# Four small constants' loads moved in SP's order, and a head selector made on ScalarE, in an RWKV-7 layer

## The chip, the core and the metric

The kernel runs on one core of a Trainium2 chip (trn2). The metric is device time in microseconds for one execution, lower is better. Engines are named as in the profile: PE is TensorE, ACT ScalarE, DVE VectorE, POOL GpSimd, and SP the sync engine, whose queue issues nearly all of this kernel's DMAs.

## The reference, cut to what matters

One decoder layer over 2048 tokens of width 1024, in float32: RWKV-7 time mixing with 12 heads of 64, beside a 4-head cross-attention into 256 memory tokens, then a squared-ReLU MLP of width 4096.

```python
h = rms_norm(x, norm_mix_g)
proj = h @ rw_in                                   # (2048, 2816)
slab = token_shift(proj[..., :2560], rw_mu)        # z + (z_prev - z) * mu
r, k, v, wd, ad, gd = split(slab)
...                                                # decay, a, g by small loras; kk normalised per head
y = delta_rule_scan(r, decay, k, v, -kk, kk * a)   # 2048 steps, 12 heads
mix = (group_norm(y) + bonus) * g
mem_out = memory_cross_attention(q_mem, k_mem, v_mem, ...)
x = x + concat([mix, mem_out]) @ w_out
x = x + square(relu(rms_norm(x, norm_ffn_g) @ w_ff1)) @ w_ff2
```

## The kernel before

Tokens come in four groups of 512 and in 16 pairs of chunks of 64. `project(g)` (L633) brings a group's x in four tiles of 128 rows, normalises them (`rows_norm`, L148: a square with its sum on ACT, L151; a reciprocal root on POOL, L86; a scaling on DVE, L153), transposes them on PE (L161) and splits them into a high and a low part, `xh` on ACT (L92) and `xl` on DVE (L93). It then multiplies with the 22 blocks of 128 columns of `rw_in`: 24 matmuls of 128 x 512 for a block (L102, three for each of eight slices of the inner width). For the first group, the weights of a block come as four loads `ws` (L604), are scaled by the gain `gmc` and split into `w` (ACT L95, DVE L96), and are stored for the later groups as `w_d` (L609). The buffers of `w` hold two blocks, so the split of block b waits for the matmuls of block b - 2.

A finished block `pz` leaves PSUM in `shift_store` (L666): ACT scales it by `omc` = 1 - mu (L674), DVE adds the shifted part with `muc` = mu (L675) and keeps the last column (L680), and the result `sl` is stored as `rk_d` (L682). The pool `psx` that holds `pz` has three banks, and the transposes of the memory tokens (`memory_setup`, L710: tiles `mt`, transposed as `pt`, split as `mh` and `ml`) take banks of the same pool in between. After five blocks stand the projections of the memory tokens to keys and values, `pk` (L628), with weights `wo` scaled by `gm`.

The constants: `gmc`, `gm` and `gfc` (L170) are gains of 1024 values, loaded as 128 partitions of 8 single values; `muc` (L575) is 2560 values as 128 partitions of 20, and `omc` is made of it on DVE (L577). `gm` is first needed by the memory weights, `gfc` by the MLP's rows (L849). The head selector `sel2` (12 heads by 768 columns, in three parts at partitions 96, 64 and 0) is written in `scan_setup` on POOL: a memset of one and two selections for each part (L231 to L235). The identity `ident` is made on POOL too. `sel2` is first read by a matmul at L356, in the first pair's preparation.

The order on each engine is set by a scheduler that runs over the whole program: it takes what is ready on its own estimate of times, lowest rank (`tc.cur_priority`) first, so one moved rank can change the order of much that follows. The DMAs that SP issues use eight completion semaphores in turn: in the program, a DMA's issue also waits until the one eight places ahead of it has landed.

Of the kernel before, what the change touches and what calls it, by code (L numbers as in the profile page):

```python
# [13 lines left out]
ALU = mybir.AluOpType  # L14
# [11 lines left out]
MW = 768  # L26
NB = MW // P
NH = 12
HD = 64
# [31 lines left out]
def hybrid_layer(  # L61
# [6 lines left out]
    nc = tc.nc  # L68
# [7 lines left out]
    ident = cst.tile([P, P], F32, name="ident")  # L76
# [91 lines left out]
    def gain_col(pool, src, name):  # L168
        t = pool.tile([P, KB], F32, name=name)
        nc.sync.dma_start(t, src.rearrange("(k p) -> p k", p=P))  # L170
        return t
# [17 lines left out]
    def col(src, name):  # L189
        t = cb.tile([P, NB], F32, name=name)  # L190
        nc.sync.dma_start(t, src.rearrange("(b p) -> p b", p=P))
        return t
# [3 lines left out]
    heads = lambda a: a.rearrange("p (h d) -> p h d", d=HD)  # L196
# [4 lines left out]
    def scan_setup():  # L201
        K["kkc"] = col(rw_k_k[0], "kkc")
        kac = col(rw_k_a[0], "kac")
        K["lbc"] = col(rw_lnx_b[0], "lbc")
        K["ka2"] = ka2 = cb.tile([P, NB], F32, name="ka2")
        nc.vector.tensor_scalar_mul(ka2, kac, 0.5)
        K["ka1"] = ka1 = cb.tile([P, NB], F32, name="ka1")
        nc.vector.tensor_scalar(ka1, kac, -0.5, 1.0, ALU.mult, ALU.add)
        K["lgr"] = lgr = cb.tile([P, MW], F32, name="lgr")
        nc.sync.dma_start(lgr, rw_lnx_g.to_broadcast([P, MW]))  # L210

        K["lora"], K["lob"] = [], []
        for which, (w2, w0) in enumerate(((rw_w2, rw_w0), (rw_a2, rw_a0))):
            src = pr.tile([P, MW], F32, tag="kk", name="lsrc")
            for o in range(2):
                nc.sync.dma_start(src[o * HD : (o + 1) * HD], w2[0])
            wt = cb.tile([P, MW], F32R, name=f"lora{which}")
            lo = pr.tile([P, MW], F32R, tag="EM", name="llo")
            nc.scalar.copy(wt[:HD], src[:HD])
            nc.scalar.copy(lo[HD:], src[HD:])  # L220
            nc.vector.tensor_tensor(wt[HD:], src[HD:], lo[HD:].bitcast(F32), op=ALU.subtract)
            K["lora"].append(wt)
            b0 = col(w0[0], f"lob{which}")
            nc.vector.tensor_scalar_mul(b0, b0, 0.5)
            K["lob"].append(b0)

        K["sel2"] = sel2 = cb.tile([96 + NH, MW], BF16, name="sel2")
        nc.gpsimd.memset(sel2, 0.0)
        for o in PARTS:
            so = sel2[o : o + NH]  # L230
            nc.gpsimd.memset(so, 1.0)  # L231
            nc.gpsimd.affine_select(so, so, pattern=[[1, MW]], compare_op=ALU.is_ge,
                                    fill=0.0, base=0, channel_multiplier=-HD)
            nc.gpsimd.affine_select(so, so, pattern=[[-1, MW]], compare_op=ALU.is_ge,
                                    fill=0.0, base=HD - 1, channel_multiplier=HD)  # L235
        K["rn3"] = rn3 = cb.tile([96 + NH, P], BF16, name="rn3")
        nc.gpsimd.memset(rn3, 0.0)
        K["g2s"] = g2s = cb.tile([P, MW], F32, name="g2s")
        nc.sync.dma_start(g2s, rw_g2[0])
        K["rkm"] = rkm = cb.tile([P, NB, 2], F32, name="rkm")  # L240
        nc.vector.memset(rkm, 0.0)
        rk_src = rw_r_k[0].rearrange("(b two) d -> two d b", two=2)
        nc.sync.dma_start(rkm[:HD, :, 0], rk_src[0])
        nc.sync.dma_start(rkm[HD:, :, 1], rk_src[1])

        K["sel1"] = sel1 = cb.tile([P, NB * NH], F32, name="sel1")
        nc.vector.memset(sel1, 0.0)
        nc.vector.memset(sel1[:HD, 0 : 14 * NB - 13 : 14], 1.0)
        nc.vector.memset(sel1[HD:, 1 : 14 * NB - 12 : 14], 1.0)

        K["msk"] = msk = cb.tile([P, P], F32, name="msk")
        nc.gpsimd.memset(msk, 1.0)
        nc.gpsimd.affine_select(msk[:HD, :C], msk[:HD, :C], pattern=[[1, C]], compare_op=ALU.is_ge,
                                fill=0.0, base=-1, channel_multiplier=-1)
        nc.gpsimd.affine_select(msk[:HD, C:], msk[:HD, C:], pattern=[[1, C]], compare_op=ALU.is_ge,
                                fill=0.0, base=0, channel_multiplier=-1)
        nc.sync.dma_start(msk[HD:], msk[:HD])
        K["rst"] = rst = cb.tile([P, 2 * P], F32, name="rst")
        nc.vector.memset(rst, 1.0)
        nc.vector.memset(rst.rearrange("p (a c) -> p a c", c=C)[:, :, 0], 0.0)  # L260

        zrow = K["zrow"] = dram.tile([2, 512], F32, name="zrow")
        ztmp = pr.tile([1, 512], F32, tag="zt", name="ztmp")
        for par in range(2):
            nc.vector.memset(ztmp, 0.0)
            nc.vector.memset(ztmp[:, par : 512 : 34], 1.0)
            nc.sync.dma_start(zrow[par : par + 1], ztmp)
        K["E"] = cb.tile([P, NB, 2, C + 1], F32, name="E")

        K["Z"] = [cb.tile([P, NB, 2 * C], F32, name=f"Z{i}") for i in range(3)]  # L270
        K["te2"] = [cb.tile([P, NB, 32], F32, name=f"te2{i}") for i in range(2)]
        nc.vector.memset(K["E"][:, :, :, 0], 1.0)
        for t in K["Z"] + K["te2"]:
            nc.gpsimd.memset(t, 0.0)
        S = st.tile([P, NB, HD], F32, tag="S", name="S")
        nc.vector.memset(S, 0.0)
        return S
# [291 lines left out]
    wp = astk.enter_context(tc.tile_pool(name="a_w", bufs=WBUF))  # L569
    ep = astk.enter_context(tc.tile_pool(name="a_e", bufs=2))  # L570
    gmc = gain_col(xp, g_mix[0], "gmc")
    gm = gain_col(xp, g_mem, "gm")
    gfc = gain_col(xp, g_ffn[0], "gfc")
    muc = xp.tile([P, 20], F32, name="muc")
    nc.sync.dma_start(muc, rw_mu[0].rearrange("(b p) -> p b", p=P))  # L575
    omc = xp.tile([P, 20], F32, name="omc")
    nc.vector.tensor_scalar(omc, muc, -1.0, 1.0, ALU.mult, ALU.add)  # L577
    last = [xp.tile([P, 20], F32, name=f"last{i}") for i in range(2)]

    w_d = [dram.tile([P, WQ, 2, KB // WQ, P], F32, name=f"w_d{b}") for b in range(NPB)]  # L580
# [278 lines left out]
    for _ in mixed(project(0), memory_setup(), 184, 21):  # L859
        pass  # L860
    S = scan_setup()
    rank["base"] = tc.cur_priority
    nxt = prepare(0)
# [357 lines left out]
```

## Time and profile before

| | |
|---|---|
| runs | 2703.28, 2704.94, 2721.36 us, median 2704.94 |
| the profiled execution | 2706.92 us, of which the span of its instructions 2705.2 us |
| PE busy | 2578.1 us (95%) |
| DVE / ACT / POOL busy | 1800.2 / 1344.5 / 233.9 us (67 / 50 / 9%) |
| mean granted clock of PE, of full speed | 0.967 |
| DMA | 523.45 MB, mean 193 GB/s |

PE's busy time includes modelled ends of matmuls. Idle time of an engine is given with what released it, as in `[2.44 <-DVE ml L93]`: 2.44 us idle until DVE had made `ml`. A DMA's row on SP (SPq) is the time that its issue took; the time to landing is told apart from it.

### The profile page before, as it was taken

To read this page: it belongs to the slowest core of one execution; us is meant where nothing else is said; L and a number is where in the kernel's file an instruction comes from. 1 tells how busy PE (TensorE), PEld (TensorE's weight loads), DVE (VectorE), ACT (ScalarE), POOL (GpSimd) and SP (SyncE) were. 2 spreads that over 40 slices of the span, in tenths; PEclk is the share of its full clock that TensorE was granted. 3 is DMA by queue.
4 is the path that set the end of the run, shared out by engine and by line. 5 is a ranking of instruction groups with operands and counts; after the bars stand their busy time and mean duration, and the time that the engine had idled before them with its cause. 6 is when DMAs were issued, how large, how long until landed. Compare 5 with 4: busy or idle time off the path is not lost.

```text
span 2705.2 us, 48412 instructions
## 1 busy us (share of the span) xinstructions
PE 2578.1 (95%) x17236; PEld 2093.3 (77%) x17236; DVE 1800.2 (67%) x4564; ACT 1344.5 (50%) x2909; POOL 233.9 (9%) x180
## 2 busy tenths in 40 slices
PE   6989999999999998899789999999999999999999
PEld 4777777777777777788667888888888888888887
DVE  4556677767775767788485777765866666655564
ACT  4563355545544646473653444455744555544443
POOL 2000021201111111111210000000000000000000
PEclk9999999999889998899899999999999999999999
DMA  8987665645465454445475677896775444456674
GB/s 246 293 271 207 169 198 144 191 135 171 129 169 137 132 159 127 113 122 165 149 269 192 236 242 269 282 318 197 246 256 171 136 159 144 168 189 210 210 257 164
DMA packets 453989, 523.45 MB, mean 193 GB/s; under 512 B 118450, under 2 KB 263922, under 8 KB 453748
## 3 DMA queue, kind: packets, MB, share of 16 engines
q1 hardware_dynamic: 452596, 516.18, 61.2%
q0 software_dynamic: 1152, 4.19, 0.4%
q8 instruction: 135, 2.21, 0.3%
q14 instruction: 106, 0.87, 0.1%
HBM read 361.87 MB, written 158.34 MB: 192 GB/s over the span
## 4 chain that ended last, share of the span: by engine, by line
PE 75%; DMA 9%; DVE 7%; ACT 4%; issue 2%; SPq 2%; POOL 1%; DVEq 0%; ACTq 0%; POOLq 0%
PE py L1108 22%; PE pu L999 18%; PE pz L102 14%; PE pout L628 3%; PE pp L391 2%; PE px L1154 2%; DMA ws<-in_w_ff_dram 1%; PE py L520 1%; DVE zt L429 1%; DVE Zw L433 1%; PE py L526 1%; PE prhs L483 1%; PE pw L489 1%; PE pe L464 1%; PE pe L457 1%
## 5 line engine op out<-in xcount | busy, mean ns | idle before, releaser
L102 PE MATMUL pz<-xh,w 128*128 128x512 f32 x1408 | 486.7, 415 | 3.7 <-ACT pe_m L780 1.7
L1108 PE MATMUL py<-wpl,hhh 128*128 128x512 f32 x896 | 349.0, 389 | 0.0
L1108 PE MATMUL py<-wph,hhl 128*128 128x512 f32 x896 | 348.8, 389 | 0.0
L1108 PE MATMUL py<-wph,hhh 128*128 128x512 f32 x896 | 344.7, 391 | 0.0
L102 PEld LDWEIGHTS pz<-xh,w 128*128 128x128 f32 x1408 | 270.3, 194 | 71.5 <-issue 6.2
L93 DVE TENSOR_TENSOR hhl<-hr,hhh 128x512 fp32r<-128x512 f32 x224 | 154.4, 689 | 215.0 <-ACT hhh L92 214.7
L102 PE MATMUL pz<-xl,w 128*128 128x512 f32 x704 | 289.8, 412 | 0.0
L92 ACT CAST hhh<-hr 128x512 fp32r<-128x512 f32 x224 | 139.5, 623 | 301.8 <-PE py L1108 283.7
L429 DVE TENSOR_TENSOR zt<-Ti,Zw 96x96 f32<-96x96 f32 (+20 forms) x736 | 161.3, 242 | 51.7 <-DMA Ti<-nd 36.9
L1108 PEld LDWEIGHTS py<-wph,hhl 128*128 128x128 f32 x896 | 168.2, 188 | 34.9
L1108 PEld LDWEIGHTS py<-wph,hhh 128*128 128x128 f32 x896 | 168.1, 188 | 34.8 <-ACT wph L92 0.2
L1108 PEld LDWEIGHTS py<-wpl,hhh 128*128 128x128 f32 x896 | 168.2, 188 | 34.5
L433 DVE TENSOR_TENSOR Zw<-Zw,zt 96x96 f32<-96x96 f32 (+20 forms) x736 | 158.2, 237 | 6.4
L102 PEld LDWEIGHTS pz<-xl,w 128*128 128x128 f32 x704 | 136.7, 194 | 30.9 <-issue 2.7
L93 DVE TENSOR_TENSOR wpl<-wr,wph 128x512 fp32r<-128x512 f32 x224 | 153.4, 685 | 4.7 <-ACT wph L92 4.7
L92 ACT CAST wph<-wr 128x512 fp32r<-128x512 f32 x224 | 138.1, 616 | 14.3 <-PE pu L999 6.5
L628 PE MATMUL pout<-wo,xh 128*128 128x256 f32 x512 | 111.5, 307 | 7.6 <-ACT wo L92 6.6
L391 PE MATMUL pp<-AR,BK 64*128 64x128 f32 x768 | 94.7, 317 | 21.1 <-DVE PT L393 19.2
L391 PEld LDWEIGHTS pp<-AR,BK 64*128 64x128 f32 x768 | 78.4, 211 | 38.4 <-DVE PT L393 23.2
L393 DVE TENSOR_TENSOR PT<-pp,msk 128x384 f32<-128x384 f32 x128 | 67.7, 549 | 45.3 <-PE pp L391 45.3
L628 PEld LDWEIGHTS pout<-wo,xh 128*128 128x128 f32 x512 | 87.4, 203 | 13.2 <-ACT wo L92 7.7
L1154 PE MATMUL px<-wx,mxh 128*128 128x512 f32 x256 | 84.2, 407 | 13.0 <-DVE wx L93 9.5
(305 smaller groups left out, 5580.6 us busy)
## 6 DMA issues: line engine op xcount, KB each, us to landing
w<-w_d SPq DMA_DIRECT2D x264, 256.0 KB, 4.0
hr<-hc_d SPq DMA_DIRECT2D x224, 256.0 KB, 2.8
ws<-in_w_ff_dram SPq DMA_DIRECT2D x32, 1024.0 KB, 6.6
hc_d<-hs SPq DMA_DIRECT2D x128, 256.0 KB, 2.3
wr<-t_d SPq DMA_DIRECT2D x128, 256.0 KB, 3.4
wr<-in_w_ff_dram SPq DMA_DIRECT2D x96, 256.0 KB, 3.4
w_d<-w SPq DMA_DIRECT2D x88, 256.0 KB, 4.2
hc_d<-h SPq DMA_DIRECT2D x64, 256.0 KB, 3.3
```

Source lines behind the costliest of these rows:

```text
L92: nc.scalar.copy(hi, src)
L93: nc.vector.tensor_tensor(lo, src, hi.bitcast(F32), op=ALU.subtract)
L102: nc.tensor.matmul(ps, a(k), b(k), start=(k == 0 and i == 0), stop=(k == nk - 1 and i == 2))
L391: nc.tensor.matmul(pps[q][:, j, :], BK[c][rs, b, :], d["AR"][rs, b, :], start=True, stop=True)
L393: nc.vector.tensor_tensor(PT[:, q * NB + 3 * hb : q * NB + 3 * hb + 3, :], pps[q], K["msk"].unsqueeze(1).to_broadcast([P, 3, 2 * C]), op=A ...
L429: nc.vector.tensor_tensor(zt[:, j0:j1, :nt], Ti[:, s, s + 1 :].unsqueeze(1).to_broadcast([96, j1 - j0, nt]), Zw[:, j0:j1, s : s + 1].to_br ...
L433: nc.vector.tensor_tensor(Zw[:, j0:j1, s + 1 :], Zw[:, j0:j1, s + 1 :], zt[:, j0:j1, :nt], op=ALU.add)
L457: nc.tensor.matmul(pe[lo, b, :], d["PT"][:32, q * NB + b, 32:C], te[:, q * NB + b, :], start=True, stop=True)
L628: nc.tensor.matmul(po[:, t, :], a(k, t), w[k][:, b], start=(k == 0 and i == 0 and t == 0), stop=(k == KB - 1 and i == 2 and t == 1))
L999: nc.tensor.matmul(ps, a[u][:, k * P : (k + 1) * P], b[v][:, k, :], start=(first and k == 0 and i == 0), stop=(k == 3 and i == 2), skip_gr ...
L1108: nc.tensor.matmul(ps[bk], a[u][:, m * P : (m + 1) * P], b[v], start=(fresh and c == 0 and t == 0), stop=(c == NCH - 1 and t == 2), skip_g ...
L1154: nc.tensor.matmul(ps[m], ops[k][u][:, m * P : (m + 1) * P], b[v], start=(k == 0 and i == 0), stop=(k == KB - 1 and i == 2))
```

## The change

Two edits. The loads of `gm`, `gfc` and `muc`, and `omc` on DVE, get a rank 2000 higher (later) than before; `gmc` stays. And the three parts of `sel2` are written by one ACT copy each, from the identity's first 12 rows and columns, each column repeated 64 times, in place of a memset and two selections on POOL.

```diff
         K["sel2"] = sel2 = cb.tile([96 + NH, MW], BF16, name="sel2")
         nc.gpsimd.memset(sel2, 0.0)
         for o in PARTS:
-            so = sel2[o : o + NH]
-            nc.gpsimd.memset(so, 1.0)
-            nc.gpsimd.affine_select(so, so, pattern=[[1, MW]], compare_op=ALU.is_ge,
-                                    fill=0.0, base=0, channel_multiplier=-HD)
-            nc.gpsimd.affine_select(so, so, pattern=[[-1, MW]], compare_op=ALU.is_ge,
-                                    fill=0.0, base=HD - 1, channel_multiplier=HD)
+            nc.scalar.copy(heads(sel2[o : o + NH]), ident[:NH, :NH].unsqueeze(2).to_broadcast([NH, NH, HD]))
...
     gmc = gain_col(xp, g_mix[0], "gmc")
+
+    tc.cur_priority += 2000
     gm = gain_col(xp, g_mem, "gm")
     gfc = gain_col(xp, g_ffn[0], "gfc")
     muc = xp.tile([P, 20], F32, name="muc")
     nc.sync.dma_start(muc, rw_mu[0].rearrange("(b p) -> p b", p=P))
     omc = xp.tile([P, 20], F32, name="omc")
     nc.vector.tensor_scalar(omc, muc, -1.0, 1.0, ALU.mult, ALU.add)
+    tc.cur_priority -= 2000
```

What that does to the order is shown at three places. Lines of the changed kernel are 2 lower than before in this part of the program (L637 is the old L639), 5 lower in `scan_setup` and what follows it.

SP from its first instruction, before:

```order
L639 DMA xt<-in_x_dram 128x1024 x4
L170 DMA gmc<-in_norm_mix_g_dram 128x8x1
L170 DMA gm<-in_mem_norm_g_dram 128x8x1
L170 DMA gfc<-in_norm_ffn_g_dram 128x8x1
L575 DMA muc<-in_rw_mu_dram 128x20x1
L604 DMA ws<-in_rw_in_dram 128x2x128 x4
L715 DMA qk<-in_mem_q_norm_g_dram 128x64
L716 DMA qk<-in_mem_k_norm_g_dram 128x64
L723 DMA mt<-in_mem_dram 128x1024
```

and now:

```order
L637 DMA xt<-in_x_dram 128x1024 x4
L170 DMA gmc<-in_norm_mix_g_dram 128x8x1
L602 DMA ws<-in_rw_in_dram 128x2x128 x4
L713 DMA qk<-in_mem_q_norm_g_dram 128x64
L714 DMA qk<-in_mem_k_norm_g_dram 128x64
L721 DMA mt<-in_mem_dram 128x1024
```

Three loads of single values have left the place between `gmc` and the first weights.

SP where the weights of the fifth block are stored (`w_d_161`; `w_d_157` to `w_d_161` are blocks 0 to 4, `rk_d_67` the results of the first group), before:

```order
L609 DMA w_d_161<-w 128x512
L604 DMA ws<-in_rw_in_dram 128x2x128
L422 DMA Zw<-zrow 48x512
L609 DMA w_d_161<-w 128x512
L604 DMA ws<-in_rw_in_dram 128x2x128
L682 DMA rk_d_67<-sl 128x512
L422 DMA Zw<-zrow 48x512
L609 DMA w_d_161<-w 128x512
L604 DMA ws<-in_rw_in_dram 128x2x128
L639 DMA xt<-in_x_dram 128x1024
L616 DMA ws<-in_w_mem_kv_dram 128x2x256 x4
L682 DMA rk_d_67<-sl 128x512 x2
```

and now:

```order
L607 DMA w_d_161<-w 128x512
L602 DMA ws<-in_rw_in_dram 128x2x128
L417 DMA Zw<-zrow 48x512 x2
L607 DMA w_d_161<-w 128x512
L602 DMA ws<-in_rw_in_dram 128x2x128
L572 DMA muc<-in_rw_mu_dram 128x20x1
L680 DMA rk_d_67<-sl 128x512 x3
L637 DMA xt<-in_x_dram 128x1024
L614 DMA ws<-in_w_mem_kv_dram 128x2x256 x4
L680 DMA rk_d_67<-sl 128x512 x2
```

`muc` stands here now, behind the last weights of the fifth block, and the first three stores of results stand behind it together. `gm` and `gfc` stand 27 and 24 rows further up. On ACT the first three scalings by `omc` stand together likewise, behind all the splits of the fifth block.

PE at the third group of transposes of memory tokens, before (60 projection matmuls stand ahead of it):

```order
L102 MATMUL pz<-xl,w 128x512
L102 MATMUL pz<-xh,w 128x512
L161 MATMUL pt<-ident,mt 128x128 x4
L102 MATMUL pz<-xh,w 128x512
L102 MATMUL pz<-xl,w 128x512
```

and now (72 stand ahead of it, three whole blocks):

```order
L102 MATMUL pz<-xl,w 128x512
L102 MATMUL pz<-xh,w 128x512
L161 MATMUL pt<-ident,mt 128x128 x4
L102 MATMUL pz<-xh,w 128x512
L102 MATMUL pz<-xl,w 128x512
L102 MATMUL pz<-xh,w 128x512 x2
```

The group has moved 12 matmuls back, from the middle of the third block to its end; the groups before it and the fourth, after 92 matmuls, stand where they stood.

## Rows read from the trace of the kernel before

**Rows 1.** Busy time by stretch, core 0; the first row names the columns.

```profile
core 0: us, PE busy (x) PEld busy (x) DVE busy (x) ACT busy (x) POOL busy (x), PEclk, DMA share, GB/s
...
58.00:61.00 3.00, 3.00 (x10) 2.23 (x9) 2.89 (x6) 2.18 (x5) 0.00 (x0) 0.50 0.96 322
...
74.50:78.20 3.70, 3.70 (x31) 3.61 (x30) 3.18 (x13) 2.86 (x10) 0.00 (x0) 0.97 0.64 194
...
180.00:1400.00 1220.00, 1131.85 (x10863) 909.42 (x10862) 852.14 (x2920) 622.47 (x1571) 202.81 (x132) 0.93 0.57 163
```

**Rows 2.** Chain that ended last, 0 to 130 us: start, us, what.

```profile
61.65 6.38 DMA xt<-in_x_dram
...
78.42 40.01 PE pz L102 x171
```

**Rows 3.** SP's own timeline: start, us of issue, line, out<-in, count.

```profile
3.41 1.28 SPq L170 DMA_DIRECT2D gm<-in_mem_norm_g_dram  x1
4.74 4.21 SPq L170 DMA_DIRECT2D gfc<-in_norm_ffn_g_dram  x1
...
9.61 3.24 SPq L604 DMA_DIRECT2D ws<-in_rw_in_dram  x4
...
14.35 0.94 SPq L604 DMA_DIRECT2D ws<-in_rw_in_dram  x2
...
61.12 0.42 SPq L604 DMA_DIRECT2D ws<-in_rw_in_dram  x1
```

**Rows 4.** DMA issues of 0 to 14 us: count, KB, us to landing.

```profile
gm<-in_mem_norm_g_dram SPq DMA_DIRECT2D x1, 4.0 KB, 6.5
...
muc<-in_rw_mu_dram SPq DMA_DIRECT2D x1, 10.0 KB, 3.8
```

**Rows 5.** Timeline of POOL in the first 20 us.

```profile
4.81 2.28 POOL L231 MEMSET sel<- 12x768 bf16 x3
...
7.45 0.54 POOL L86 TENSOR_TENSOR nr<-nm,nhalf 128x1 f32<-128x1 f32 x1
```

**Rows 6.** Timeline of ACT: start, us, what, [idle before <-releaser].

```profile
4.55 1.06 ACT L151 ACTIVATE junk<-xt 128x1024 bf16<-128x1024 f32 x1 [2.47 <-DMA xt<-in_x_dram]
...
13.56 0.69 ACT L95 ACTIVATE w<-ws,gmc 128x128 fp32r<-128x128 f32 x2 [6.49 <-DMA ws<-in_rw_in_dram]
...
38.22 0.84 ACT L219 CAST lora<-lsrc 64x768 fp32r<-64x768 f32 x1 [4.07 <-DMA lsrc<-in_rw_w_dram]
...
41.75 0.67 ACT L674 ACTIVATE sl<-pz,omc 128x512 f32<-128x512 f32 x1
```

**Rows 7.** Timeline of DVE, in the same form.

```profile
8.02 1.41 DVE L153 TENSOR_SCALAR xt<-xt,nr 128x1024 f32<-128x1024 f32 x1 [2.14 <-POOL nr L86]
...
12.82 0.62 DVE L577 TENSOR_SCALAR omc<-muc 128x20 f32<-128x20 f32 x1 [3.33 <-DMA muc<-in_rw_mu_dram]
...
59.01 0.75 DVE L675 SCALAR_TENSOR_TENSOR sl<-pz,muc,sl 128x511 f32<-128x511 f32 x1
```

**Rows 8.** Timeline of PE, in the same form.

```profile
29.33 0.79 PE L102 MATMUL pz<-xh,w 128*128 128x512 f32 x1 [0.34 <-ACT xh L92]
...
50.01 0.63 PE L102 MATMUL pz<-xh,w 128*128 128x512 f32 x2
...
57.53 1.04 PE L161 MATMUL pt<-ident,mt 128*128 128x128 f32 x4 [2.44 <-DVE ml L93]
58.22 1.20 PE L102 MATMUL pz<-xh,w 128*128 128x512 f32 x2
...
61.48 0.40 PE L102 MATMUL pz<-xl,w 128*128 128x512 f32 x1
...
65.93 0.40 PE L102 MATMUL pz<-xh,w 128*128 128x512 f32 x1
...
78.14 0.28 PE L628 MATMUL pk<-wo,ml 128*128 128x256 f32 x1
```

## The prediction

> **What bounds the kernel now.** I read three views in turn. The busy time by stretch comes first: from 180 to 1400 us PE is busy 1131.9 of 1220 us [rows 1], so 88 us are lost there, spread over many short waits. In the first 80 us, which this change touches, the loss has one cause. The second view is the chain of work that ended last: up to 68 us it runs almost wholly through SP and the DMAs that SP issues (its last such piece is the load of x that SP issues at 61.65 us and that lands 6.38 us later), and from 78.42 us on it is PE, 40 us in one piece [rows 2]. The third view is SP's own timeline. From 14.35 us to the end of the weight load at 61.12 + 0.42 us stand 69 DMAs; their issues alone last 38.3 us (summed over the rows between those two), the rest is short waits [rows 3]. So SP is a queue that is nearly always full: 47.2 us for 69 DMAs, 0.68 us each. Whatever stands late in that queue comes late, however small it is.
>
> **Part 1: the loads leave the front of SP.** Now gm's issue takes from 3.41 us (1.28 us) and gfc's from 4.74 us (4.21 us); muc follows, and the first weights start at 9.61 us [rows 3]. After, they start at 3.4 us. The fifth weight load goes out at 14.35 us now; in the changed program its issue waits for gmc to have landed, the DMA eight places ahead of it. gm took 6.5 us from issue to landing [rows 4], and gmc is issued 0.75 us ahead of gm and stands behind the same four loads of x. I take gmc as landed at 8.5 us (between 7.2 and 9.2) and the fifth weight load at 8.8 us: SP's stream is then 5.5 us ahead (5.0 to 6.9).
>
> On ACT the first weights are split at 13.56 us, after 6.49 us of idle time waiting for them, and only behind that, in ACT's order, comes the third tile of x [rows 6]. With gmc landed at 8.5 us and the first weights about 1 us behind it, ACT has no such wait: 16 weight splits of 0.33 us, 8 splits of x of 0.57 us and three squares of 1.2 us make 13.5 us of work from 9.5 us on. The first projection matmul, now at 29.33 us [rows 8], would come at about 23 us (22 to 25).
>
> **Part 2: the selections leave POOL.** Three memsets (2.28 us together from 4.81 us) and six selections stand there now, and the first reciprocal root waits behind the memsets until 7.45 us [rows 5]; DVE sat idle 2.14 us for it, and its first scaling of x took 1.41 us beside POOL's work [rows 7]. That is about 1 us on the way to the first transposes. In its place ACT gets three copies of 12 x 768 ahead of the first square. The trace has no such copy; the nearest row is the cast of 64 x 768 at 0.84 us [rows 6]. Bounds for one: 0.57 us (128 x 512) to 1.06 us (128 x 1024). I take 0.84, three make 2.5 us from 2.3 us (when the identity is ready) to 4.8 us; the first square, now at 4.55 us, starts 0.3 us later (0 to 1 us). The two nearly cancel, and both lie ahead of what follows: without that cover they would be worth 1 us at most.
>
> **Part 3: muc comes late, and three PSUM banks wait for it.** This is the step on which the sign rests. Every block of the projection leaves its bank through a scaling by omc, made from muc, and the pool has three banks. In the changed order muc stands behind the whole weight set of the fifth block (b = 4). PE's third group of memory transposes stands after 72 projection matmuls, where before it stood after 60: three full blocks hold all three banks, and nothing on PE can go on until the first one is scaled.
>
> When is muc issued? Between the fifth weight load and muc stand 68 DMAs: the 69 from above, less three stores of results, plus gm and gfc. I charge the 66 at the present pace, 45.1 us, and gm and gfc at 1.3 us each (gm's issue; gfc's 4.21 us is the upper bound, the 0.55 us of a mean issue, 38.3 / 69, the lower). 45.1 + 2.6 = 47.7 us, from 8.8 us: **muc is issued at 56.5 us** [rows 3]. With every wait of SP gone (68 x 0.55 = 37.7 us) it would be 46.5 us; with gfc at its present price 59.4 us.
>
> From there: 3.8 us to landing [rows 4], 0.6 us for omc, 0.67 us for the scaling on ACT, 0.75 us for the shift on DVE [rows 6, 7], 0.15 us for the column kept, some 0.4 us for the hand-overs; then 0.9 us for the same of the second block, whose bank the fourth block takes. That is 7.3 us, so the fourth block starts at 63.8 us. PE's 72nd matmul now comes at 50.01 us, 20.7 us after the first [rows 8]; after it comes at about 43.5 us. **PE then stands idle for some 19 us.**
>
> The Trainium skill (DMA: Bandwidth & Descriptors, Anatomy of one DMA) fits about 2.0 us plus bytes over 436 GB/s for a DMA issued from GpSimd. By it muc's 10 KB, though issued from SP, would take 2.0 us, and the sum would come out 1.8 us lower, at 2708; the trace's 3.8 us for this very load says otherwise, and I keep 3.8.
>
> From the idle time PE comes back at the low clock: after its present wait of 2.44 us the granted clock was 0.50 from 58 to 61 us [rows 1], 1.2 GHz, and eight matmuls took from 58.22 to 61.48 us, 0.41 us each, against 0.234 us later (19 from 61.48 to 65.93 us) [rows 8]. Blocks four and five are 48 matmuls: 10 at 0.41, 38 at 0.234, and 0.6 us of transposes, 13.6 us. They end at 77.4 us. The 48 matmuls of the memory keys, by then with their weights split (gm lands long before), take 31 in 3.7 us as from 74.5 to 78.2 us [rows 1]: 6.1 us with the two others between them. That ends at 83.5 us, where it ends at 78.4 us now (last row at 78.14 us, 0.28 us long) [rows 8]. **Sum: 5.5 us won at the front, given back, and 5.1 us lost.** From here on PE is the chain, and hands the loss on.
>
> **Part 4: the rest of the order.** The scheduler's order changes on PE up to its last 5575 of 13,622 instructions, all the way to the late output. No single step of that can be priced from the trace; I bound it by the 88 us that PE loses from 180 to 1400 us, of which I let a sixth come or go: 15 us either way, with 0 as the value taken since the counts of work are the same.
>
> **Time.** The profiled execution took 2706.92 us (span 2705.2), 2.0 above the median of 2704.94. 2706.9 + 5.1 is 2712.0 for its own; for the median, 2710.
>
> **Rivals.**
> (a) SP runs faster than now, since its waits on PE's progress fall away. Then muc goes out as early as its place allows: behind the split of the fifth block, which needs matmul 72. 43.5 us + 1.9 us for split, store and load + 7.3 us puts the fourth block at 52.7 us and the end of the memory keys at 72.4 us, **6.0 us faster, 2699**. For it: 9 of the 47.2 us are waits. Against it: each DMA also waits for the one eight ahead of it; at 3.8 to 6.5 us from issue to landing [rows 4] that alone gives 0.5 to 0.8 us a DMA. It is faster than before once muc is issued ahead of 51 us.
> (b) The new order costs a part of the middle stages: one more wait of 1 us on PE in each of the 16 pairs of chunks, on top of part 3, gives 2704.94 + 5.1 + 16 = **2726**. For it: 88 us of such waits are there already and the clock is 0.93 [rows 1]. Against it: every rank in that stretch is as before.
> (c) The new order saves there: a sixth of the 88 us less the loss of part 3 gives 2704.94 - 15 + 5.1 = **2695**. The same for and against.
>
> **Chances.** Forecast (late muc decides, 2704 to 2717): 0.5; (a) 0.2; (b) and beyond 0.17; (c) and beyond 0.13. The range of 8 in 10 reaches from (c) to just past (b): 2695 to 2728, some 0.1 left on either side. What a measurement can tell from no change is about 1%, 27 us: past 2732 lie the ends of (b), 0.07; under 2678 the ends of (c), 0.04; within it 0.89.
>
> **What would show it.** Part 1: gm and gfc gone from SP's first 10 us, first projection matmul at 22 to 25 us. Part 2: three casts on ACT before the first square, the first reciprocal root at 6.4 us. Part 3: muc's issue at 56 to 57 us, PE idle some 19 us with DVE's shift or kept column as what ended it, a granted clock near 0.50 behind it, and the memory keys done at 83 to 84 us. If muc is issued before 51 us, or PE's wait there is under 11 us, part 3 is wrong and (a) holds. If the keys end there and the total still differs by more than 5 us from the forecast, part 4 is where it went, and busy time from 180 to 1400 us shows it.

## The result, and the profile after

The changed kernel takes 2744.7 us (median; 2740.0 to 2751.0) against 2709.6 us for the kernel before on the same chip. The ratio is 1.013, with a 95% interval of 1.0097 to 1.0163: **slower by about 35 us**. The forecast was 5 us slower, with a range that ended at 2728 us.

| | before | after |
|---|---|---|
| span of the profiled execution | 2705.2 us | 2749.3 us |
| TensorE busy | 2578.1 us | 2596.1 us |
| TensorE idle (span less busy) | 127.1 us | 153.2 us |
| mean granted clock | 0.967 | 0.958 |
| VectorE / ScalarE busy | 1800.2 / 1344.5 us | 1788.1 / 1346.2 us |

Of the 44 us between the two profiled spans, 26 are idle time of TensorE and 18 are busy time: the same 17236 matmul records, at a lower granted clock.

The front ended as forecast. SyncE's queue after (start, time of the issue):

```profile
3.44 4.47 SPq L602 DMA_DIRECT2D ws<-in_rw_in_dram  x4
...
10.51 2.99 SPq L602 DMA_DIRECT2D ws<-in_rw_in_dram  x6
...
35.87 0.41 SPq L170 DMA_DIRECT2D gm<-in_mem_norm_g_dram  x1
...
38.54 0.51 SPq L170 DMA_DIRECT2D gfc<-in_norm_ffn_g_dram  x1
...
56.13 0.57 SPq L572 DMA_DIRECT2D muc<-in_rw_mu_dram  x1
```

Against [rows 3] gm and gfc are gone from the first 10 us and the weights start at 3.44 us instead of 9.61. The fifth weight load goes out at 10.51 us instead of 14.35, and muc is issued at 56.13 us.

TensorE after (start, duration, what, and in brackets the idle time before it with what ended that):

```profile
23.55 0.78 PE L102 MATMUL pz<-xh,w 128*128 128x512 f32 x1
...
45.84 0.39 PE L102 MATMUL pz<-xh,w 128*128 128x512 f32 x1
...
62.65 1.09 PE L161 MATMUL pt<-ident,mt 128*128 128x128 f32 x4 [16.42 <-DVE last L678]
63.39 0.78 PE L102 MATMUL pz<-xh,w 128*128 128x512 f32 x1
...
82.54 0.40 PE L626 MATMUL pk<-wo,mh 128*128 128x256 f32 x2
```

The first projection matmul comes 5.8 us earlier than in [rows 8], the 72nd ends at 46.2 us, then TensorE waits 16.42 us until VectorE has kept the last column of the first block. The memory keys end at 82.9 us, against 78.4 before. The chain of waits of that place shows muc's transfer alone between the queue and the scaling:

```profile
56.13 4.60 DMA muc<-in_rw_mu_dram
60.73 0.02 issue
60.76 0.19 DVE omc L574
60.95 0.02 issue
60.97 0.70 ACT sl L672
```

Busy time by stretch after, with the columns of [rows 1]:

```profile
45.00:62.60 17.60, 1.23 (x6) 0.65 (x4) 6.89 (x21) 7.31 (x19) 0.55 (x1) 0.63 0.85 215
62.60:66.00 3.40, 3.35 (x10) 2.89 (x11) 2.04 (x5) 0.80 (x2) 0.00 (x0) 0.50 0.60 231
...
180.00:1400.00 1220.00, 1125.75 (x10765) 899.83 (x10763) 819.54 (x2893) 605.75 (x1543) 200.62 (x130) 0.92 0.54 156
```

Behind the wait the clock is 0.50 (1.2 GHz), the lower of the two levels, as in [rows 1]. From 180 to 1400 us TensorE gets through 10765 matmuls instead of 10863, at 0.92 instead of 0.93. The memory keys end 4.5 us late and the program 44 us late in these two profiles, so most of the loss arises behind the front. The longest groups of TensorE's waits between 900 and 1460 us, first before, then after (us in total, times, longest):

```profile
PE px L1154 <- DVE wx L93: 9.5, 5, 3.4
PE pe L464 <- ACT Z L465: 8.0, 6, 4.8
PE pp L391 <- DVE PT L393: 7.8, 5, 2.6
PE pout L628 <- ACT wo L92: 6.6, 3, 3.7
```

```profile
PE pout L626 <- ACT wo L92: 14.1, 4, 8.7
PE pp L386 <- DVE PT L388: 11.7, 6, 5.4
PE pt L844 <- DVE xt L153: 8.6, 3, 6.4
PE px L1152 <- ACT wx L92: 5.9, 1, 5.9
```

The same kinds of waits, but single ones of 5 to 9 us where before none was above 4.8. `pout` is the output projection, `pp` a product of the scan's preparation, `pt` a transpose of the MLP's rows, `px` the late output.

### The profile page after: what moved, and what is told of

Read it like the earlier page. It is cut to its first block, busy times and chain, and to the rows that moved or that the text cites. A ratio compares the mean times of both kernels' runs of the same rounds, so it can differ in the third digit from the quotient of the medians.

```text
span 2749.3 us, 48411 instructions
## 1 busy us (share of the span) xinstructions
PE 2596.1 (94%) x17236; PEld 2103.5 (77%) x17236; DVE 1788.1 (65%) x4564; ACT 1346.2 (49%) x2912; POOL 225.9 (8%) x171
## 4 chain that ended last, share of the span: by engine, by line
PE 75%; DMA 10%; DVE 8%; ACT 3%; issue 2%; SPq 2%; POOL 1%; DVEq 0%; ACTq 0%; POOLq 0%
PE py L1106 22%; PE pu L997 18%; PE pz L102 14%; PE pout L626 3%; PE px L1152 3%; PE pp L386 2%; DMA KT<-rk_d 1%; DMA ws<-in_w_ff_dram 1%; PE py L515 1%; PE pw L484 1%; PE pe L452 1%; PE pb L411 1%; PE py L521 1%; PE prhs L478 1%; PE psco L769 1%
## 5 line engine op out<-in xcount | busy, mean ns | idle before, releaser
L424 DVE TENSOR_TENSOR zt<-Ti,Zw 96x96 f32<-96x96 f32 (+20 forms) x736 | 153.3, 233 | 54.8 <-DMA Ti<-nd 45.6
L626 PE MATMUL pout<-wo,xh 128*128 128x256 f32 x512 | 115.7, 316 | 17.8 <-ACT wo L92 14.1
L386 PE MATMUL pp<-AR,BK 64*128 64x128 f32 x768 | 98.8, 318 | 21.0 <-DVE PT L388 20.1
```

Of the source, the lines that this page charges most:

```text
L386: nc.tensor.matmul(pps[q][:, j, :], BK[c][rs, b, :], d["AR"][rs, b, :], start=True, stop=True)
L424: nc.vector.tensor_tensor(zt[:, j0:j1, :nt], Ti[:, s, s + 1 :].unsqueeze(1).to_broadcast([96, j1 - j0, nt]), Zw[:, j0:j1, s : s + 1].to_br ...
L626: nc.tensor.matmul(po[:, t, :], a(k, t), w[k][:, b], start=(k == 0 and i == 0 and t == 0), stop=(k == KB - 1 and i == 2 and t == 1))
```

## The experiments

The theories: **1**, the scheduler's new order behind the front costs some 30 us and the late muc 5; **2**, the late front costs all of it, in whatever order; **3**, the copies on ScalarE cost it; **4**, any new order is a draw, unrelated to what the edit is for. In the results, "us over before" is the ratio less 1, times 2707 us; a thousandth in an interval is 2.7 us.

### Front and rest apart

To hold one part of the order fixed, every engine's instructions were chained in a written list, taken from the scheduled programs of the two kernels. The chain orders the issue only and adds no wait:

```diff
+    pin_order(tc)     # at the end of hybrid_layer
+def pin_order(tc):
+    for steps in lists:                  # one list for each engine
+        for prev, ins in pairs(steps):
+            tc.add_manual_dep(ins, prev.name, NoSync, reason="pin_order")
```

In the traces the pinned stretches show the order that was asked for on every engine, but for the seams and a few neighbouring matmuls that changed places. **frontA_restB** has the changed kernel's source and order for what the kernel before starts up to 85 us, and the order of before from there. **frontB_restA** is the mirror image.

> The changed kernel with the issue order of every engine written out by hand: its own order for everything that the kernel before has started by 85 us (597 to 636 instructions, the late loads and the copies among them), and from there the order of the kernel before. Theory 1 (the new order behind 85 us costs 30 to 40 us, the late gains only the 4.6 us that the memory keys end later): 5 us over the kernel before, 2709 to 2718 us, with the waits of 14.1 us in the output stage and of 8.6 us in the late output gone. Theory 2 (the 4.6 us of the front grow downstream in whatever order): 30 to 40 us over the kernel before, 2735 to 2750 us.

> The mirror image: the kernel before, with its own order up to 85 us (loads early, selections on GpSimd), and from there the order of the changed kernel on every engine. Theory 1 (the order behind 85 us): 30 to 40 us over the kernel before, 2735 to 2750 us, TensorE idle about 20 us more than before. Theory 2 (the front): as the kernel before, 2700 to 2715 us.

Measured: frontA_restB 1.0021 (0.9997 to 1.0046), 6 us over before (-1 to 12), though its TensorE stands idle 17.12 us for muc:

```profile
61.42 1.09 PE L358 MATMUL pt<-ident,mt 128*128 128x128 f32 x4 [17.12 <-DVE last L875]
```

frontB_restA 1.0107 (1.0056 to 1.0158), 29 us over before (15 to 43), with no late load in it; its TensorE idles 15 us more than before, where about 20 were expected. Theory 1 gave both times within their errors; theory 2 falls. frontB_restA also shows the changed kernel's waits again (TensorE's waits, 900 to 1460 us):

```profile
PE pout L825 <- ACT wo L289: 14.4, 4, 8.8
PE pp L588 <- DVE PT L590: 12.9, 7, 5.4
PE pt L1043 <- DVE xt L350: 9.5, 4, 6.4
PE px L1351 <- ACT wx L289: 5.9, 1, 5.9
```

The order alone makes them: 14.4 against 14.1 us, 9.5 against 8.6, 5.9 against 5.9.

### The two edits apart

**loads_late_only** is the changed kernel with the selections back on GpSimd, **copies_only** the kernel before with the three copies:

```diff
-            nc.gpsimd.affine_select(so, ...)    # memset and two selections for each part
+            nc.scalar.copy(heads(sel2[o : o + NH]), ident[:NH, :NH].unsqueeze(2).to_broadcast([NH, NH, HD]))
```

> The loads ranked late, the selections left on GpSimd, the scheduler free. Its order behind the front is a third one (on TensorE an instruction stands 21 places from where it stood before and 11 from where the changed kernel has it, on average). Theory 1 with no rule for what an order costs (theory 4, a draw): 5 us for the front and anything from -10 to +40 for the order, 2700 to 2750 us. Theory 2: 2735 to 2750 us. Theory 3 (the three copies on ScalarE are what costs): 5 us over before, 2709 to 2718 us.

> The three copies on ScalarE alone, the loads as before, the scheduler free. On TensorE its order stands 20 places from that of before on average, nearly as far as the changed kernel's 25, though the front has no late load. Theory 4 (a draw): -10 to +40 us against before, with the front up to 80 us as before. Theory 2: as before, 2700 to 2715 us. Theory 3: 30 to 40 us over before.

Measured: loads_late_only 1.007 (1.0045 to 1.0094), 19 us over before; copies_only 1.0007 (0.998 to 1.0034), no measurable difference (-5 to 9 us). Theory 3 falls. The late loads, 6 us with the old order behind them, cost 19 with the scheduler free and 35 together with the copies.

### Where along the way

> The order of the kernel before for everything that it has started by 1000 us (some 9,960 of 23,304 instructions), and from there the order of the changed kernel. In the run with only the front of before, the lag against before was 4 us lower at 900 us, 6 us at 1000 us and 29 us behind 1450 us. Theory 1a (what the new order costs is paid behind 1000 us, in the stretch with the output projection, the feed-forward rows and the late output): 20 to 28 us over before, 2727 to 2736 us. Theory 1b (it is paid before 1000 us, or only with both halves together): 0 to 10 us over before, 2705 to 2717 us.

> The mirror image: the changed kernel's order for what the kernel before has started by 1000 us, with the late loads and the copies, and from there the order of before. Theory 1a: the front's 5 us and what the first 1000 us add (the lag was 18 us at 1000 us in the changed kernel, part of it instructions that only stand elsewhere): 5 to 15 us over before, 2710 to 2722 us. Theory 1b: 30 to 40 us over before, 2735 to 2748 us.

> The kernel before with the changed kernel's order only for what stands between 1000 and 1300 us (the output projection of the second quarter, beside the scan), and its own order ahead of that and behind it. With the changed order from 1000 us to the end it took 23 us more; its lag in the trace was 10 us at 1200 us, 21 us at 1300 us and 29 us behind 1450 us. If the stretch from 1000 to 1300 us costs by itself: 10 to 20 us over before, 2717 to 2731 us. If the cost arises behind 1300 us, where the late output starts 40 us later on TensorE: 0 to 6 us over before, 2705 to 2717 us.

> The kernel before with the changed kernel's order only for what stands between 1000 and 1150 us. With the whole stretch to 1300 us changed it took 25 us more; its lag in the trace was 6 us by 1150 us, and the 8 us wait for a split output weight ends at 1150 us. One costly place (that wait and what it drags along): 15 to 25 us over before, and nothing in the other half. Many places that add up: 5 to 12 us over before here, 12 to 20 in the other half.

> The other half: the changed kernel's order only for what stands between 1150 and 1300 us. One costly place ahead of it: 0 to 5 us over before. Many places that add up: 12 to 20 us over before, so that both halves together come to 25 give or take 7. The cost needs the whole stretch: both halves within 6 us of before.

| changed kernel's order | ratio | us over before |
|---|---|---|
| from 1000 us on (B1000_thenA) | 1.0087 (1.0057 to 1.0116) | 24 |
| up to 1000 us, with the late loads (A1000_thenB) | 1.008 (1.0055 to 1.0105) | 22 |
| 1000 to 1300 us only | 1.0099 (1.0064 to 1.0134) | 27 |
| 1000 to 1150 us only | 1.0041 (1.0025 to 1.0057) | 11 |
| 1150 to 1300 us only | 1.0109 (1.0084 to 1.0134) | 30 |

The part behind 1000 us costs its 24 us within 1000 to 1300 us (27), and nothing that these errors resolve later, though the late output starts 40 us later (1396 us in frontB_restA, 1356 us in before). Three expectations were too low: the part ahead of 1000 us was expected at 5 to 15 us and took 22, of which 6 are the front; the stretch from 1000 to 1300 us at 10 to 20 and took 27; its second half at 12 to 20 and took 30.

In the trace of A1000_thenB VectorE's instructions stand 6.2 us later than in before at 900 us (median of the 50 us from there) and 19.5 us later at 1000 us, where the order is that of before again, so what this part adds to the front is lost mostly between 900 and 1000 us.

The parts don't add up: 11 and 30 make 41 where the whole stretch takes 27. 24 and 22 make 46 where the whole kernel takes 35, which is within the errors. A change of order in the middle of a program also makes a seam of its own: A1000_1300_only waits 4.56 us for `lin` at 1021 us, where frontB_restA waits 0.5.

What the loss is made of shows in the busy time of about the same 3260 matmuls, before from 1000 to 1330 us:

```profile
1000.00:1330.00 330.00, 293.72 (x3276) 254.44 (x3270) 249.44 (x842) 174.12 (x461) 56.90 (x37) 0.90 0.46 131
```

and with the changed order from 1150 to 1300 us:

```profile
1000.00:1353.00 353.00, 310.02 (x3254) 266.60 (x3252) 246.85 (x835) 174.25 (x461) 58.56 (x38) 0.85 0.43 122
```

Of 23 us only 6.7 are more idle time (353 less 310.02, against 330 less 293.72); 16.3 are busy time at a clock of 0.85 instead of 0.90, and 293.72 x 0.90 / 0.85 is 311. But some 7 of the 23 us are not the changed order's. Up to 1150 us both traces have the same order on every engine, and in the same 30 us of it, with TensorE busy throughout, the clock differs; before, then with the changed order from 1150 us:

```profile
1060.00:1090.00 30.00, 30.00 (x351) 24.95 (x350) 21.04 (x74) 18.24 (x53) 2.49 (x2) 0.87 0.39 110
```

```profile
1060.00:1090.00 30.00, 30.00 (x262) 25.09 (x260) 13.64 (x46) 13.43 (x40) 2.49 (x2) 0.60 0.32 92
```

Both idled 7.9 us in the 30 us ahead of that. Seven traces have the order of before there (also frontA_restB, front500_restB, mucfront_restB, scanA_outB and scanB_outA), and their clock in these 30 us lies between 0.55 and 0.94, on one chip as on several. So it goes with the single execution and not with the order. From 1150 us in before, and from 1156 us with the changed order, which lies 6 us behind by then:

```profile
1150.00:1330.00 180.00, 161.22 (x1994) 144.35 (x1991) 135.76 (x488) 95.21 (x253) 30.98 (x22) 0.93 0.48 136
```

```profile
1156.00:1353.00 197.00, 172.02 (x2003) 152.05 (x2001) 135.28 (x496) 96.43 (x256) 32.64 (x23) 0.88 0.44 124
```

That is 17 us more, 6.2 of idle and 10.8 of busy time.

Other runs split otherwise: over the whole span A1000_1300_only has 16.4 us more idle and 6.9 us more busy time than before, B1000_thenA 18.3 and 10.9, frontB_restA 15.4 and 13.8. And rank500 has 18.8 us less idle and 20.1 us more busy time in a span 1.3 us longer, at a mean clock of 0.966 against 0.967, so the split between idle and busy time doesn't price the clock by itself.

Two pieces of 30 us from the place where the order changes, before and then with the changed order (6 us behind, so not quite the same matmuls):

```profile
1140.00:1170.00 30.00, 25.98 (x307) 23.17 (x309) 21.14 (x99) 13.19 (x36) 1.01 (x1) 0.83 0.39 107
1170.00:1200.00 30.00, 29.88 (x402) 26.47 (x399) 22.30 (x75) 20.38 (x53) 1.56 (x2) 1.00 0.43 118
```

```profile
1140.00:1170.00 30.00, 21.71 (x217) 18.91 (x217) 17.02 (x87) 10.90 (x30) 1.01 (x1) 0.71 0.46 123
1170.00:1200.00 30.00, 27.73 (x383) 23.91 (x384) 20.54 (x72) 17.43 (x44) 0.00 (x0) 0.84 0.32 77
```

Where TensorE idles 8.3 us instead of 4.0, the granted clock is 0.71 instead of 0.83, and it is still 0.84 in the next 30 us, in which TensorE is busy 92% of the time. The idle time goes with a lower clock for the busy time beside it and behind it; how far behind differs from one execution to the next, as the rows of 1060 to 1090 us show.

### One wait taken away

The longest wait of frontB_restA is for a weight of the output projection. In SyncE's queue its load stands seven places further back than before, behind stores that wait for VectorE. **frontB_restA_ws** puts 21 transfers of that queue back into the order of before:

```diff
-  x2 store, SG, mix_d, zdr, zdr, Ti, Ti, mem_d, ws, Z x8, Zw x2, ws, ws, ws
+  x2 store, ws, mem_d, SG, mix_d, zdr, zdr, Ti, Ti, ws, ws, ws, Z x8, Zw x2
```

> The run with the front of before and the changed kernel's order behind 85 us, with 21 transfers of SyncE's queue put back into the order of before: the load of one output weight and the three behind it stand again next to the store that precedes them, instead of 7 to 18 places further on, behind stores that wait for VectorE. There TensorE idled 8.85 us until ScalarE had split that weight (3.7 us in before). Theory 1c (the order costs through such queues, each wait its own length and the clock after it): that wait falls to 3 to 5 us and the time by 5 to 10 us, 2727 to 2733 us. Theory 1d (the next instruction on TensorE waits for something as late): the wait moves to the next tile and the time stays within 2 us of 2738 us.

Measured: 1.0126 (1.0095 to 1.0156), 34 us over before and no gain against 1.0107. TensorE in frontB_restA, then with the load put back, then VectorE in the first and in the second:

```profile
1153.24 0.58 PE L825 MATMUL pout<-wo,xh 128*128 128x256 f32 x1 [8.85 <-ACT wo L289]
1153.75 0.84 PE L654 MATMUL pe<-te,PT 32*32 32x32 f32 x12
```

```profile
1154.05 0.38 PE L825 MATMUL pout<-wo,xh 128*128 128x256 f32 x1 [3.10 <-ACT wo L289]
1163.21 0.84 PE L654 MATMUL pe<-te,PT 32*32 32x32 f32 x12 [8.78 <-DVE te L648]
```

```profile
1152.97 0.76 DVE L648 STREAM_TRANSPOSE te<-Z 32x192 f32<-32x192 f32 x2 [8.46 <-DMA Z<-zdr]
```

```profile
1162.79 0.77 DVE L648 STREAM_TRANSPOSE te<-Z 32x192 f32<-32x192 f32 x2 [11.72 <-DMA Z<-zdr]
```

The wait for the weight falls to 3.10 us and the next product, one matmul later, waits 8.78 us for the scan's solve, whose result goes through DRAM (`zdr` out, `Z` back) and reaches VectorE after 11.72 us. In the kernel before, 25 matmuls of the output projection stand ahead of the product where here stands one, and it starts without a wait (TensorE before):

```profile
1143.51 1.04 PE L628 MATMUL pout<-wo,xh 128*128 128x256 f32 x2 [3.69 <-ACT wo L92]
...
1149.39 0.77 PE L457 MATMUL pe<-te,PT 32*32 32x32 f32 x12
```

So behind the late weight stood a second wait of the same length, as theory 1d had it: in frontB_restA VectorE waited 8.46 us for `Z`, until 1152.97 us, and the weight's matmul came at 1153.24. In the edited queue that wait is 3.3 us longer; the stores of `zdr` and the loads of `Z` now stand behind weight loads that followed them. The place of that one load doesn't explain the loss.

### Other orders for almost nothing

**rank500** ranks the loads 500 behind instead of 2000, **muc_early** leaves muc at its old rank, **gfc_late_only** moves nothing but gfc's load, in the kernel before:

```diff
+    tc.cur_priority += 2000
     gfc = gain_col(xp, g_ffn[0], "gfc")
+    tc.cur_priority -= 2000
```

> The changed kernel with its loads ranked 500 behind instead of 2000: gm, gfc and muc then stand at places 21, 26 and 29 of SyncE's queue, behind the first weights but ahead of the constants of the scan, so that muc lands well before the first shift; the scheduler is free. Theory 1 with 4 (the order behind the front is a draw): no wait of 16 us in the front, the first 80 us 4 to 6 us shorter than in the changed kernel by the keys' end, and the total anywhere from 2695 to 2745 us. Theory 2 (the late muc is what costs): 2695 to 2706 us.

> The changed kernel with muc left at its old rank (place 5 of SyncE's queue), gm and gfc late, copies on ScalarE, the scheduler free. Theory 2 and the prediction's rival with muc in time: 2697 to 2706 us. Theory 4 (each new order is a draw; so far 2, 6, 17 and 35 us over before): no wait of 16 us in the front and anything from -5 to +35 us against before, 2700 to 2745 us.

> The kernel before with one change: the load of gfc, 4 KB that nothing reads before the feed-forward rows behind 1000 us, ranked 2000 behind; the scheduler is free. The transfer itself can bring or cost a microsecond at most (one issue less ahead of the first weights). On TensorE an instruction stands 28 places from where it stood before, on average. Theory 4: anything from -5 to +35 us. A theory by which only the edit's own work counts: within 3 us of before, 2704 to 2712 us.

Measured: rank500 1.0018 (0.9994 to 1.0042), 5 us over before; muc_early 1.005 (1.0032 to 1.0069), 14; gfc_late_only 1.0044 (1.0023 to 1.0065), 12. None of the three has the wait of 16 us for muc. gfc_late_only moves a 4 KB load that is not read ahead of 1000 us, and costs 12 us. With the changed kernel, loads_late_only and copies_only these are six schedules of nearly the same work: 2, 5, 12, 14, 19 and 35 us over before. The front explains little of that order: the two slowest have the late muc, worth some 6 us. That is as theory 4 has it, but six schedules of which none is faster don't show a draw.

### The edit with the order held

**front500_restB** and **mucfront_restB** take the fronts of rank500 and of muc_early up to 85 us, and then the order of before.

> The front of that kernel (rank 500, muc in time, copies on ScalarE) up to 85 us, and from there the order of before, written out. What the edit can give if no order changes behind it: the rival with muc in time came to 6 us under before. The lag of 5 us of the changed front was no longer to be seen behind 1000 us in its profile, so a lead may be lost in the same way. Theory 1: 2696 to 2708 us.

> The front with muc at its old place (fifth in SyncE's queue), gm and gfc late and the copies on ScalarE, and from 85 us the order of before, written out. The prediction's rival for this front came to 6 us under before, 2699 us. The front with rank 500 and the same rest took 4.5 us less than before. If the front's gain lasts to the end: 2699 to 2704 us where before stands at 2705 to 2708. If it is lost on the way: within 2 us of before.

Measured: front500_restB 0.9974 (0.9953 to 0.9995), 7 us faster than before and the fastest of all; mucfront_restB 0.9988 (0.9974 to 1.0003), within the error of before. With muc in time and no other order behind it, the edit gives something between nothing and 13 us. In the trace of mucfront_restB, VectorE's instructions of 75 to 100 us come 3.3 us earlier than before (median); whether such a lead lasts to the end is less than these runs resolve.

### Two halves of one order

Among the first 60 scan matmuls behind 1150 us before starts 64 matmuls of the output projection and the memory attention, and A1150_1300_only 11 (behind 1156 us). So the changed order lets the scan run ahead and leaves the filling work for later. Two kernels take one half each.

> The kernel before; only between 1150 and 1300 us are the steps of the scan (preparation, scan, closing) put among themselves into the changed kernel's order. The work that fills in beside them (output projection, memory attention) keeps its own order and its places among them. If the placing of the filling work is what costs: 0 to 8 us over before, 2706 to 2715 us. If the order among the scan's steps is: 20 to 30 us over before, 2727 to 2738 us.

> The complement: between 1150 and 1300 us the scan's steps stand in the order of before, and the filling work stands among them where the changed kernel has it, some 80 matmuls later. If the placing of the filling work costs: 20 to 30 us over before, 2727 to 2738 us, with the output projection 30 to 40 us late in the middle of the stretch. If the order among the scan's steps does: 0 to 8 us over before.

Measured: 1.0167 (1.0124 to 1.021) and 1.0161 (1.0096 to 1.0227), some 45 and 44 us over before. Both expectations fail: one of the two should have cost little, and neither does better than the changed order whole (30 us; the intervals overlap). So these runs can't price the placing of the filling work and the order of the scan's steps apart. scanA_outB, for the matmuls of the rows above:

```profile
1001.00:1384.00 383.00, 343.13 (x3288) 283.27 (x3287) 250.72 (x844) 176.45 (x466) 59.24 (x38) 0.85 0.39 113
```

Idle time is 39.9 us, 3.6 more than before; the 53 us lost are nearly all busy time at 0.85. The clock's ratio accounts for 17 of them, of which some 7 fall between 1060 and 1090 us, where the order is still that of before (clock 0.55 in this run); what else lengthened the matmuls stays open.

## Why the prediction was wrong

**Part 1 held at both ends and missed in between.** First weights at 3.44 us (3.4), first projection matmul at 23.55 us (about 23). But the fifth weight load went out at 10.51 us, not 8.8: the first four weight loads took 4.47 us to issue instead of 3.24, and gmc landed 7.6 us after its issue, at 10.3 us (7.2 to 9.2). SyncE was 3.8 us ahead there, outside the 5.0 to 6.9 that were put down.

**Part 2 held.** The three copies took 2.51 us together (2.5), the first square started at 4.75 us instead of 4.55, the first reciprocal root at 6.17 (6.4), and the first scaling took 0.75 us instead of the 1.41 of [rows 7]. ScalarE and VectorE after:

```profile
2.33 2.51 ACT L230 CAST sel<-ident 12x768 bf16<-12x768 f32 x3 [0.25 <-POOL ident masks.py:199]
4.75 1.05 ACT L151 ACTIVATE junk<-xt 128x1024 bf16<-128x1024 f32 x1
```

```profile
6.75 0.75 DVE L153 TENSOR_SCALAR xt<-xt,nr 128x1024 f32<-128x1024 f32 x1 [0.67 <-POOL nr L86]
```

In copies_only this edit alone, with the order that the scheduler then made, changed the time by no more than its error.

**Part 3 held.** muc issued at 56.13 us (56.5), idle 16.4 us (19; TensorE's 72nd matmul ended at 46.2 us, later than the 43.5 put down), fourth block from 63.4 us (63.8), clock 0.50 behind it, keys done at 82.9 us (83.5), so 4.5 us lost (5.1). frontA_restB puts the price of this front at 6 us over the whole run (-1 to 12). That muc's issue was met to 0.4 us is partly luck. The stretch behind the fifth weight load began 1.7 us late (part 1) and was 2.1 us shorter than the 47.7 put down (45.6), mostly because gm and gfc cost 0.41 and 0.51 us of issue there, not 1.3 each. muc's transfer took 4.60 us, not 3.8. The Trainium skill (DMA: Bandwidth & Descriptors, Anatomy of one DMA) fits about 2.0 us plus bytes over 436 GB/s for a DMA issued from GpSimd, an estimate of 2.0 us for muc's 10 KB; this trace, with the issue from SyncE, shows more than twice that.

**Part 4 failed, and it decided.** "With 0 as the value taken since the counts of work are the same" and "a sixth come or go: 15 us either way" were the two steps. frontB_restA, with everything of part 4 and nothing of parts 1 to 3, costs 29 us. Three things were wrong in it:

- The bound was taken from idle time alone. Of the profiled 44 us, 18 are busy time, at a lower clock, and in A1150_1300_only from 1150 us on 10.8 of 17. The 88 us of idle time say nothing about those.
- A sixth of the present idle time was no bound at all: idle time can come anew. Behind the first 85 us, in which TensorE was busy 57.76 us before and 50.81 us after, it rose by 19 us, from 99.9 to 119.0.
- The value 0 treated the order of before as a middling one. Six free schedules of nearly the same work came out between 2 and 35 us over before (copies_only and rank500 within their error of it) and none measurably faster, so before stood at the good end of these, and a new order was a loss of 14.5 us on average (87 / 6). Why it stood there is not shown.

Rival (b), 16 us for the reorder, named the right place at about half the size. Its form, one more wait of 1 us in each pair, is not what the waits show: they are single ones of 5 to 9 us, with a lower clock beside them. Its argument against ("every rank in that stretch is as before") didn't hold: the ranks were the same and the order wasn't. Rival (a) did not happen: muc was issued at 56.13 us, not before 51. With muc in time and the order held, its 6 us lie within the intervals of both runs, mucfront_restB (3 us faster, -7 to 1) and front500_restB (7 us faster, -13 to -1); with the scheduler free muc_early is 14 us slower. The last test that the prediction named is what showed it: the keys ended where forecast, and the total differed from the forecast by 35 us.

What stays open: which places of the changed order, between 900 and 1000 us above all, cost the 16 us that it adds to the front ahead of 1000 us, and which rule tells a good order of scan and filling work from a bad one. The runs exclude the one late weight load, and mixing the two halves of the order did not tell them apart. The differences between single profiles carry some 7 us of chance: A1150_1300_only lies 1.6 us ahead of before at 1000 us and 6.0 behind at 1050 us (VectorE, median of the 50 us from there), in the same order of issue, which is the stretch of 1060 to 1090 us with its clock of 0.60 instead of 0.87.

## What to carry to other kernels

Where a scheduler orders a whole program, the price of an edit is its own work plus that of a new order, and the second can be the larger: measure both by writing the old order out behind the edit. A reorder of a stretch that runs at 93% busy and a clock of 0.93 is not free because the work is the same, and its idle time is no bound for the cost: idle time can come anew, and the clock of the busy time beside it can fall too. Compare many executions before a difference of 7 us between two profiles is read as the edit's. A load that is first read late is only cheap to move if its place in a full queue is ahead of its use: rank it behind the first weights (rank500), not behind everything.

## What the hardware showed that was not expected

- The issue of the same load took 4.21 us as one of the first DMAs [rows 3] and 0.51 us at 38.5 us (gfc), 1.28 and 0.41 us (gm). The four weight loads that took gfc's place at the front took 4.47 us for four, against 3.24 us behind it. So a long issue at the start of this program goes with the place in the queue, or with what stands ahead of it there, and not with the load alone.
- A copy of 12 x 768 on ScalarE took 0.83 us (2.51 us for three), about the same as the cast of 64 x 768 of [rows 6].
- The same order gave a different clock: with TensorE busy 30.00 of 30 us, behind 7.9 us of idle time in the 30 us before, the granted clock was 0.87 in one execution and 0.60 in another (1060 to 1090 us of before and A1150_1300_only, 351 and 262 matmuls), some 7 us apart.
- More short waits cost busy time beside idle time: 6.2 us more idle time of TensorE went with 10.8 us more busy time at 0.88 instead of 0.93 of full speed (A1150_1300_only, from 1150 us on). The single wait of 16.4 us in the front left the clock at 0.50 (1.2 GHz) from 62.6 to 66 us; from 66 to 70 us it was 0.91.
